# Seven-product projections of a decoder block: two products add into another's PSUM bank, five additions instead of seven, and the first values evicted behind the rates

## The chip, the cores and the metric
The kernel runs on one core of a Trainium2 chip. Five engines work side by side, each through its own instructions in a fixed order, and wait for one another by semaphores: TensorE (PE in the profile, PEld its weight loads), VectorE (DVE), ScalarE (ACT), GpSimd (POOL) and SyncE (SP, which issues most DMAs). PE writes its products into PSUM, here used as eight banks of 128 x 512 float32; DVE and ACT read them from there. The metric is the device time of one execution in microseconds (us), and less is better.

## The reference
One layer of a decoder block, 1024 tokens by 1024 features, all float32:

```python
h = rms_norm(x, pre_mix_norm)
xr, gr, q, k, v, gates = split(h @ w_in)          # widths 1024, 1024, 3 x 1536, 2048
xr = rg_lru(causal_depthwise_conv(xr, conv_w, conv_b), ...)   # gates per block, then a scan over time
y_lru = (xr * gelu(gr)) @ w_lru_proj
q, k = partial_rope(q), partial_rope(k)            # 32 of 128 features of a head are rotated
o = softmax-weighted sum over 3 groups of dilated_window_attention(q, k, v)
y_attn = o @ w_attn_proj
g_lru, g_attn = split(sigmoid(gates))
x = x + rms_norm((g_lru * y_lru + g_attn * y_attn) @ w_out, post_mix_norm)
h = rms_norm(x, pre_ffn_norm)
f = (silu(h @ w_ffn_gate) * (h @ w_ffn_up)) @ w_ffn_down      # width 2816
return x + rms_norm(f, post_ffn_norm)
```

## The kernel before
**Precision.** A float32 operand is split into a high part that PE takes at its fast rate (`hi`, an ACT copy, L98) and the rest (`lo`, a DVE subtraction, L99). A term of a product is three matmuls (`mm3`, L133 to L135): hi by hi, lo by hi, hi by lo. In the profile weights are called `whi` and `wlo`, the layer's normed input and its combinations `hth`/`htl`, `t1`, `t3`, `t4` with h or l behind.

**Quads.** The projections onto xr, gr, q, k and the gates (28 quads, stage 1) and the FFN's gate and up (22 quads) are computed in 2 by 2 blocks with seven products instead of eight. A product is one bank `pq` of 12 matmuls of 128 x 512. The four weight blocks come in two loads (`wraw`); POOL forms their sums `sa` and `sb` (L267 to L270); P1 and P2 take their weights from the first load, P6 and P7 from `sa`, P5 and P3 from `sb`, P4 from a block of the second load (`w4h`, `w4l`). Each pair shares one tile `whi` and one `wlo`, of which there are three. ACT copies P1's bank to `p` (L294), and DVE adds up the rest: u2 = P6 + P1, w = P5 + u2, v = P7 + u2 (tiles `uw`, L309), and the outputs out(0,0) = P2 + P1, out(0,1) = P3 + w, out(1,1) = P7 + w, out(1,0) = P4 + v. An output of stage 1 is the tile `fb` (L720); where there is a function (gelu, sigmoid) ACT applies it to `fb` in place (L722). In the FFN a gate's output is `fo` (L1232, then silu on ACT), and up's is `ut` (L1238), which POOL multiplies into `fo` (L1239). `run_quads` issues a quad as P6, P5, P3, P7, P4 and then P1 and P2 of the next; after each a tick is counted.

**Work between the quads.** The ticks start other work by a table: the units of the LRU (`lru_a`: conv on DVE, L768 and L770, and its split `xch`, `xcl`; `lru_b`: gate matmuls `pgt`, functions on ACT, a scan on DVE) from tick 15 on, every 8; six rotations (`rotate`, L811 to L816; q and k rows `rq` and tables `rcs`, `rsn` come by SP from memory) from tick 146 on, every 5. The weights' second load of a quad waits on SP for its buffer, whose last reader is the split of `w4l`.

**The beginning.** The first half's mean squares (`squares`, L434) give rates (`rates`, L439 to L451: a root on ACT, six small DVE steps, four diagonals `dg`, one matmul `prb` that spreads the rates). Meanwhile the value projection of the first group runs on raw x (banks `bk0`, then `bk1`, `pv`), and `v0_out` (L479) evicts it with the rates as scale. `put` (L425, L426) makes `hth` and `htl`. The same follows for the second half. In the order of the instructions a scheduler has a say; `tc.issue_after(i)` keeps what is inside it behind instruction i on the queue's order. The rotation tables (`rope_tables`) are written to memory from tiles `rot`; the quads' tiles lie in memory that was theirs.

**The FFN's start.** `ORDER` lists steps: t (transposes of a row tile of the normed input), p (weights of a quad's P1 and P2), h (P1, P2 and the copy), x (sums of columns of the input and their splits, L563). Four quads have P1 and P2 ahead of the loop.

Of the kernel before, what the change touches and what calls it, by code (L numbers as in the profile page):

```python
# [41 lines left out]
ORDER = [(s[0], int(s[1])) for s in "t6 h1 p2 p3 x5 h0 t7 x6 x4 h2 x7 h3".split()]  # L42
# [20 lines left out]
def block(ctx, tc, a, out):  # L63
# [169 lines left out]
    class Quad:  # L233
# [47 lines left out]
        def mm(self, p):  # L281
            bank = ps("pq")
# [3 lines left out]
                        xh[:, k, :], xl[:, k, :]) for k in range(4)])  # L286
            return bank

        def start_mm(self):
            self.b = self.mm("P1"), self.mm("P2")  # L290

        def keep(self):
            self.p1 = Quad.pool.tile([128, 512], F32, name="p1", bufs=Quad.P1B)
            A.activation(self.p1, self.b[0], AF.Copy)  # L294

        def head(self):
            self.start_mm()
            self.keep()
# [6 lines left out]
        def body(self):  # L305

            def plus(bank, x):
                y = Quad.up.tile([128, 512], F32, name="uw", bufs=3)
                V.tensor_add(y, bank, x)  # L309
                return y  # L310

            u2 = plus(self.mm("P6"), self.p1)
            yield
            w = plus(self.mm("P5"), u2)
            yield
            self.out(0, 1, self.mm("P3"), w)
            yield
            bank = self.mm("P7")
            self.out(1, 1, bank, w)
            v = plus(bank, u2)  # L320
            yield
            self.out(1, 0, self.mm("P4"), v)
            if self.done:
                self.done()
            yield

    def run_quads(quads, pre, tick=None):
        quads[0].prep()
        for j in range(pre):
            quads[j].first()  # L330
        for j, q in enumerate(quads):
            if j + 1 < len(quads):
                quads[j + 1].prep()
            for _ in q.body():
                if tick:
                    tick()
            if pre <= j + 1 < len(quads):
                quads[j + 1].head()
# [1249 lines left out]
```

## Time and profile before
| | |
|---|---|
| three runs | 1749.28, 1754.31, 1753.51 us; median 1753.51 |
| the profiled execution | 1749.78 us, span 1748.0 us, granted PE clock 0.978 of full speed |
| PE busy | 1676.7 us (96%), 7748 matmuls |
| DVE busy | 1113.9 us (64%) |
| ACT busy | 727.5 us (42%) |
| POOL busy | 698.0 us (40%) |
| chain that ended last | PE 77%, DVE 8%, DMA 5% |

The span is what the profiler saw from the first instruction to the last; the device time lies 1.8 us above it. Busy shares are means over stages that differ. A wait names the engine and line whose result came last.

### The profile page before, as it was taken

Reading aid. Unit: us, or ns where it says so; the run is one execution under the profiler, and the core shown is the slowest. Engines: PE = TensorE matmul, PEld = TensorE weight load, DVE = VectorE, ACT = ScalarE, POOL = GpSimd, SP = SyncE. Lnnn points to the kernel's source line nnn. Section 1 sums busy time; section 2 is a strip of 40 time slices with the busy share of each in tenths; the row PEclk is TensorE's granted clock in tenths of the full one; section 3 lists DMA queues with packets and bytes.
Section 4 is the critical chain, followed back from the end, with each engine's and each line's share of the span. In section 5 each row is a group of like instructions: output and inputs, shape, how many; then the busy total and the mean of one; then the engine's idle time right before and its main releaser. Section 6 shows DMA issues by size and latency. Waiting matters only on the chain.

```text
span 1748.0 us, 21093 instructions
## 1 busy us (share of the span) xinstructions
PE 1676.7 (96%) x7748; PEld 1376.2 (79%) x7748; DVE 1113.9 (64%) x1585; ACT 727.5 (42%) x1130; POOL 698.0 (40%) x650
## 2 busy tenths in 40 slices
PE   8999999999999988989999999799999999999996
PEld 6897888787877876878888887678888888788885
DVE  6966676778788665563433577755545555649658
ACT  6423367554555522464451345422222222344343
POOL 2003354554445434214334204576556566400103
PEclk9899999999999999999999999899999999999998
DMA  8233433333333455584618742133222222475353
GB/s 319 73 133 113 148 133 124 135 137 129 127 133 133 139 166 179 197 330 155 229 50 304 269 162 84 49 115 133 102 103 91 103 91 103 150 261 198 109 186 121
DMA packets 95919, 262.70 MB, mean 150 GB/s; under 512 B 13768, under 2 KB 22120, under 8 KB 94408
## 3 DMA queue, kind: packets, MB, share of 16 engines
q1 hardware_dynamic: 70352, 182.49, 30.7%
q0 software_dynamic: 20352, 76.21, 11.5%
q10 hardware_dynamic: 5112, 2.66, 0.5%
q8 instruction: 61, 1.00, 0.2%
q14 instruction: 42, 0.34, 0.1%
HBM read 180.86 MB, written 80.35 MB: 149 GB/s over the span
## 4 chain that ended last, share of the span: by engine, by line
PE 77%; DVE 8%; DMA 5%; issue 4%; POOL 3%; ACT 2%; SPq 1%; ACTq 0%; DVEq 0%; POOLq 0%
PE pq L135 14%; PE pq L134 14%; PE pq L133 14%; PE pd L1334 4%; PE pd L1335 4%; PE pd L1333 4%; DMA rsn<-rtd 3%; PE py L135 2%; PE py L134 2%; PE py L133 2%; PE pv L463 2%; PE po L1017 2%; PE pv L133 1%; PE pv L135 1%; PE pv L134 1%
## 5 line engine op out<-in xcount | busy, mean ns | idle before, releaser
L135 PE MATMUL pq<-hth,wlo 128*128 128x512 f32 x448 | 179.7, 401 | 9.8 <-DVE wlo L99 9.8
L133 PE MATMUL pq<-hth,whi 128*128 128x512 f32 x448 | 179.6, 401 | 2.8 <-ACT whi L98 2.8
L134 PE MATMUL pq<-htl,whi 128*128 128x512 f32 x448 | 180.7, 403 | 0.0
L267 POOL TENSOR_TENSOR sb<-wraw 128x512 f32<-128x512 f32 x50 | 71.6, 1432 | 173.1 <-DMA wraw<-in_w_fg 92.3
L98 ACT ACTIVATE whi<-sa 128x1024 fp32r<-128x1024 f32 x50 | 53.0, 1059 | 201.5 <-PE pq L134 126.8
L1334 PE MATMUL pd<-fbl,fah 128*128 128x512 f32 x304 | 119.7, 394 | 4.5 <-DVE fbl L99 4.5
L1335 PE MATMUL pd<-fbh,fal 128*128 128x512 f32 x304 | 119.7, 394 | 0.0
L1333 PE MATMUL pd<-fbh,fah 128*128 128x512 f32 x304 | 119.3, 393 | 0.0
L98 ACT ACTIVATE whi<-wraw 128x1024 fp32r<-128x1024 f32 x67 | 70.7, 1055 | 98.2 <-PE pq L134 25.8
L135 PEld LDWEIGHTS pq<-hth,wlo 128*128 128x128 f32 x448 | 86.0, 192 | 32.1 <-DVE wlo L99 11.6
L99 DVE TENSOR_TENSOR wlo<-wraw,whi 128x1024 fp32r<-128x1024 f32 x67 | 91.6, 1367 | 26.4 <-ACT whi L98 23.7
L309 DVE TENSOR_TENSOR uw<-pq,uw 128x512 f32<-128x512 f32 x100 | 68.3, 683 | 60.2 <-PE pq L135 59.5
L133 PEld LDWEIGHTS pq<-hth,whi 128*128 128x128 f32 x448 | 86.0, 192 | 24.7 <-ACT whi L98 3.2
L134 PEld LDWEIGHTS pq<-htl,whi 128*128 128x128 f32 x448 | 85.9, 192 | 20.5
L1407 POOL TENSOR_TENSOR y<-y,gpf 128x512 f32<-128x512 f32 x16 | 25.2, 1602 | 186.9 <-ACT fah L98 109.5
L99 DVE TENSOR_TENSOR wlo<-sa,whi 128x1024 fp32r<-128x1024 f32 x50 | 70.1, 1401 | 28.6 <-ACT whi L98 28.6
L1239 POOL TENSOR_TENSOR fo<-fo,ut 128x512 f32<-128x512 f32 x44 | 60.6, 1381 | 67.1 <-DVE ut L1238 67.1
L720 DVE TENSOR_TENSOR fb<-pq,uw 128x512 f32<-128x512 f32 x84 | 67.8, 807 | 29.4 <-PE pq L135 29.0
L99 DVE TENSOR_TENSOR fal<-ar,fah 128x1024 fp32r<-128x1024 f32 (+1 forms) x41 | 50.5, 1231 | 51.5 <-ACT fah L98 51.4
L98 ACT ACTIVATE fah<-ar 128x1024 fp32r<-128x1024 f32 (+1 forms) x41 | 40.8, 995 | 100.9 <-PE pd L1334 79.5
L133 PE MATMUL pq<-t1h,whi 128*128 128x512 f32 x200 | 79.6, 398 | 0.9 <-ACT whi L98 0.9
L134 PE MATMUL pq<-t1l,whi 128*128 128x512 f32 x200 | 79.4, 397 | 0.0
(542 smaller groups left out, 4948.0 us busy)
## 6 DMA issues: line engine op xcount, KB each, us to landing
ar<-fd SPq DMA_DIRECT2D x35, 512.0 KB
qkd<-fb POOLq DMA_DIRECT2D x24, 512.0 KB, 3.6
qk<-qkd SPq DMA_DIRECT2D x24, 512.0 KB
wraw<-in_w_fg SPq DMA_DIRECT2D x24, 512.0 KB
wraw<-in_w_fu SPq DMA_DIRECT2D x24, 512.0 KB
fd<-fo POOLq DMA_DIRECT2D x11, 1024.0 KB, 4.3
wd<-in_w_dn SPq DMA_DIRECT2D x21, 512.0 KB
fd<-fs POOLq DMA_DIRECT2D x11, 768.0 KB, 5.6
```

The source lines that it names most:

```text
L98: A.activation(hi, src, AF.Copy)
L99: (le or V).tensor_sub(lo, src, f(hi))
L133: T.matmul(o, lh, rh, start=(first and i == 0), stop=False)
L134: T.matmul(o, lh, rl, start=False, stop=False)
L135: T.matmul(o, ll, rh, start=False, stop=(last and i == n - 1))
L267: G.tensor_add(sb[:, lo_], r1[:, lo_], r1[:, hi_])
L309: V.tensor_add(y, bank, x)
L720: V.tensor_add(o, half_in(bank, g), half_in(add, g))
L1239: G.tensor_mul(g, g, ut)
L1333: T.matmul(o, ah[:, ts], bh, start=(i == 0), stop=False)
L1334: T.matmul(o, ah[:, ts], bl, start=False, stop=False)
L1335: T.matmul(o, al[:, ts], bh, start=False, stop=(i == NP - 1))
```

## The change
In a quad P2 now has no bank of its own: it adds into P1's bank once ACT has copied P1, so that bank holds P1 + P2 and needs no addition. P3 adds into P5's bank after out(1,1) has read it. The DVE additions become u2 = P6 + P1, v = P7 + u2, out(1,1) = P5's bank + v, out(1,0) = P4 + v and out(0,1) = P5's bank (with P3) + u2. ACT evicts out(0,0), with its function where there is one; in up's quads DVE multiplies the bank into `fo`. The order of products is P6, P2, P5, P7, P4, the next quad's P1, P3. `ORDER` splits h into a (P1 and its copy) and b (P2). At the beginning four `issue_after` are added and one gets another anchor. PE's matmuls stay the same in number.

```diff
-ORDER = [(s[0], int(s[1])) for s in "t6 h1 p2 p3 x5 h0 t7 x6 x4 h2 x7 h3".split()]
+ORDER = [(s[0], int(s[1])) for s in "t6 a1 p2 p3 x5 a0 b1 t7 x6 x4 a2 b0 x7 a3 b2 b3".split()]
...
+        def head1(self):
+            self.b = self.mm("P1")
         def keep(self):
             self.p1 = Quad.pool.tile([128, 512], F32, name="p1", bufs=Quad.P1B)
+            A.activation(self.p1, self.b, AF.Copy)
...
+        def head2(self):
+            self.mm("P2", self.b)
         def first(self):
             if self.start:
                 self.start()
-            self.out(0, 0, self.b[1], self.p1)
+            self.out(0, 0, self.b, None)
...
     def run_quads(quads, pre, tick=None):
...
+            u2 = plus(q.mm("P6"), q.p1)
+            step()
+            if j >= pre:
+                q.head2()
+                q.first()
+                step()
+            c = q.mm("P5")
+            step()
+            v = plus(q.mm("P7"), u2)
+            q.out(1, 1, c, v)
+            step()
+            q.out(1, 0, q.mm("P4"), v)
+            step()
+            if nxt and j + 1 >= pre:
+                nxt.head1()
+                nxt.keep()
+                step()
+            q.out(0, 1, q.mm("P3", c), u2)
+            if q.done:
+                q.done()
+            step()
...
         else:
-            put(0, j)
-            w0_split(j)
+            with tc.issue_after(last_dve[0].ins):
+                put(0, j)
+                w0_split(j)
...
     r1, rb = rates(ss[1])
-    v0_out(bk0, 0, r0)
+    with tc.issue_after(last_act[0].ins):
+        v0_out(bk0, 0, r0)
...
-    for j in range(4):
-        normed(1, j, rb)
-    for j in range(4):
-        put(0, j)
+    with tc.issue_after(last_dve[0].ins):
+        for j in range(4):
+            normed(1, j, rb)
+        for j in range(4):
+            put(0, j)
...
         def up(n, u, bank, add):
             g = FO[i][:, 2 * n + u, :]
-            ut = op.tile([128, 512], F32, name="ut", bufs=UT)
-            V.tensor_add(ut, bank, add)
-            G.tensor_mul(g, g, ut)
+            if add is None:
+                V.tensor_mul(g, bank, g)
+            else:
+                ut = op.tile([128, 512], F32, name="ut", bufs=UT)
+                V.tensor_add(ut, bank, add)
+                G.tensor_mul(g, g, ut)
```

Three places show how instructions move. The first is ACT between the squares of the second half and its root `rs` (L439, after the change L436): `vs` is an eviction of the first values, `hth` a copy of `put`. Rows of before begin with -, rows after the change with +.

```order
-L479 ACTIVATE vs_393<-pv,rr_287 128x512
-L434 ACTIVATE sq,ss_172<-xn 128x1024
-L479 ACTIVATE vs_393<-pv,rr_287 128x512
-L434 ACTIVATE sq,ss_172<-xn 128x1024
-L479 ACTIVATE vs_393<-pv,rr_287 128x512
-L434 ACTIVATE sq,ss_172<-xn 128x1024
-L479 ACTIVATE vs_393<-pv,rr_287 128x512
-L434 ACTIVATE sq,ss_172<-xn 128x1024
-L425 ACTIVATE hth_120<-x 128x2x512
-L439 ACTIVATE rs_377<-ss_172,epsc 128x4
```
```order
+L422 ACTIVATE hth_120<-x 128x2x512
+L431 ACTIVATE sq,ss_172<-xn 128x1024 x2
+L422 ACTIVATE hth_120<-x 128x2x512
+L431 ACTIVATE sq,ss_172<-xn 128x1024
+L422 ACTIVATE hth_121<-x 128x2x512
+L431 ACTIVATE sq,ss_172<-xn 128x1024
+L422 ACTIVATE hth_121<-x 128x2x512
+L436 ACTIVATE rs_377<-ss_172,epsc 128x4
+L476 ACTIVATE vs_393<-pv,rr_287 128x512 x4
 L98 ACTIVATE whi<-wraw 128x1024 x2
```
The four evictions stood between the squares; they now stand behind the root, and four copies of `put` stand ahead of it instead of one.

The second is PE at the start of stage 1, where P1 and P2 of the first two quads are computed ahead of the loop. Before, the end of the first quad's P1 (bank pq_1418) and the beginning of its P2 (pq_1431):

```order
L133 MATMUL pq_1418<-hth0_120,whi_1414 128x512
L134 MATMUL pq_1418<-htl0_122,whi_1414 128x512
L135 MATMUL pq_1418<-hth0_120,wlo_1415 128x512
L133 MATMUL pq_1431<-hth1_121,whi_1414 128x512 [waits PE_49]
L134 MATMUL pq_1431<-htl1_123,whi_1414 128x512
L135 MATMUL pq_1431<-hth1_121,wlo_1415 128x512
```
After the change, the end of the second quad's P1 (pq_1437) and the beginning of the first quad's P2:

```order
L133 MATMUL pq_1437<-hth0_120,whi_1433 128x512
L134 MATMUL pq_1437<-htl0_122,whi_1433 128x512
L135 MATMUL pq_1437<-hth0_120,wlo_1434 128x512
L133 MATMUL pq_1418<-hth1_121,whi_1414 128x512 [waits Activation_49]
L134 MATMUL pq_1418<-htl1_123,whi_1414 128x512
L135 MATMUL pq_1418<-hth1_121,wlo_1415 128x512
```
P2 waited for a free bank only; now it goes into pq_1418 and waits for ACT's copy of it, and both P1 stand ahead of both P2.

The third is DVE in the last quad that has two rotations in the group from tick 146 on. `rm`, `rq`, `rsn` and `rcs` are the rotation's tiles. Before, from its second rotation's first step on:

```order
L811 TENSOR_TENSOR rm_5480<-rq_5477,rsn 128x512
L814 TENSOR_TENSOR rq_5477<-rq_5477,rcs 128x512
L720 TENSOR_TENSOR fb<-pq,uw 128x512
L99 TENSOR_TENSOR wlo<-sa,whi 128x1024
L813 TENSOR_TENSOR rq_5476<-rq_5476,rcs 128x512
L720 TENSOR_TENSOR fb<-pq,uw 128x512
L309 TENSOR_TENSOR uw<-pq,uw 128x512
L99 TENSOR_TENSOR wlo<-sb,whi 128x1024
L815 TENSOR_TENSOR rq_5476<-rq_5476,rm_5480 128x512
L99 TENSOR_TENSOR w4l<-wraw,w4h 128x512
L720 TENSOR_TENSOR fb<-pq,uw 128x512
L816 TENSOR_TENSOR rq_5477<-rq_5477,rm_5481 128x512
```
After the change, the same rotation:

```order
L814 TENSOR_TENSOR rm_5493<-rq_5490,rsn 128x512
L816 TENSOR_TENSOR rq_5489<-rq_5489,rcs 128x512
L817 TENSOR_TENSOR rq_5490<-rq_5490,rcs 128x512
L818 TENSOR_TENSOR rq_5489<-rq_5489,rm_5493 128x512
L819 TENSOR_TENSOR rq_5490<-rq_5490,rm_5494 128x512
L309 TENSOR_TENSOR uw<-pq,uw 128x512
L99 TENSOR_TENSOR wlo<-sa,whi 128x1024
L723 TENSOR_TENSOR fb<-pq,uw 128x512 x2
L99 TENSOR_TENSOR w4l<-wraw,w4h 128x512
L723 TENSOR_TENSOR fb<-pq,uw 128x512
L99 TENSOR_TENSOR wlo<-sb,whi 128x1024
L309 TENSOR_TENSOR uw<-pq,p_5487 128x512
```
The rotation's steps were mixed with the additions; they now stand together ahead of v (the first `uw`), out(1,1) and the next quad's splits.

## Rows read from the trace of the kernel before
**Rows 1.** The page, busy time of each engine with its share of the span and its instructions.
```profile
PE 1676.7 (96%) x7748; PEld 1376.2 (79%) x7748; DVE 1113.9 (64%) x1585; ACT 727.5 (42%) x1130; POOL 698.0 (40%) x650
```
**Rows 2.** Table of windows: the stretch in us, its length, then for PE, PEld, DVE, ACT and POOL the busy time and in brackets the instructions, then the granted PE clock, the DMA share and GB/s.
```profile
39.00:62.00 23.00, 16.05 (x56) 11.83 (x55) 18.00 (x28) 7.10 (x9) 0.64 (x1) 0.78 0.26 92
50.00:75.00 25.00, 25.00 (x137) 21.63 (x136) 22.91 (x24) 10.81 (x14) 1.45 (x2) 0.95 0.13 43
157.00:169.00 12.00, 8.31 (x28) 6.07 (x27) 6.05 (x7) 5.24 (x7) 7.08 (x6) 0.86 0.25 87
175.00:600.00 425.00, 417.78 (x1768) 334.09 (x1767) 324.92 (x389) 237.70 (x292) 206.56 (x168) 0.99 0.37 131
430.00:446.00 16.00, 12.38 (x42) 9.28 (x41) 10.12 (x9) 6.96 (x9) 4.45 (x5) 0.79 0.16 55
600.00:704.00 104.00, 94.16 (x381) 74.46 (x380) 57.83 (x78) 28.38 (x40) 42.89 (x43) 0.93 0.56 182
1084.00:1124.00 40.00, 28.73 (x105) 21.84 (x104) 35.10 (x34) 19.78 (x33) 26.77 (x18) 0.79 0.13 44
1160.00:1516.00 356.00, 356.00 (x1555) 291.72 (x1554) 191.89 (x205) 99.51 (x129) 215.90 (x164) 1.00 0.28 102
```
**Rows 3.** Waits of PE: line and product, what it waited for, us in all, times, the longest.
```profile
PE pq L135 <- DVE wlo L99: 11.4, 6, 4.7
PE pq L133 <- ACT whi L98: 10.0, 4, 5.7
PE pgt L133 <- ACT xch L98: 3.9, 3, 2.2
```
**Rows 4.** Groups of instructions by line and shape, of DVE and POOL: busy us and mean ns, then the idle time before them.
```profile
L309 DVE TENSOR_TENSOR uw<-pq,uw 128x512 f32<-128x512 f32 x100 | 68.3, 683 | 60.2 <-PE pq L135 59.5
L720 DVE TENSOR_TENSOR fb<-pq,uw 128x512 f32<-128x512 f32 x84 | 67.8, 807 | 29.4 <-PE pq L135 29.0
L99 DVE TENSOR_TENSOR wlo<-sa,whi 128x1024 fp32r<-128x1024 f32 x50 | 70.1, 1401 | 28.6 <-ACT whi L98 28.6
L1239 POOL TENSOR_TENSOR fo<-fo,ut 128x512 f32<-128x512 f32 x44 | 60.6, 1381 | 67.1 <-DVE ut L1238 67.1
```
**Rows 5.** Timeline of DVE, ACT and PE, 20 to 48 us: start, duration, engine, line, operation; in brackets the idle time before it and what ended it.
```profile
22.10 0.17 DVE L441 RECIPROCAL rr<-rs 128x4 f32<-128x4 f32 x1
22.97 0.87 DVE L449 TENSOR_SCALAR dg<-cst,re 128x128 f32<-128x128 f32 x4
32.14 0.69 ACT L479 ACTIVATE vs<-pv,rr 128x512 f32<-128x512 f32 x1 [5.28 <-PE pv L463]
32.73 1.05 ACT L434 ACTIVATE sq<-xn 128x1024 f32<-128x1024 f32 x1
38.60 1.06 ACT L425 ACTIVATE hth<-x 128x1024 fp32r<-128x1024 f32 x1
39.55 0.29 ACT L439 ACTIVATE rs<-ss,epsc 128x4 f32<-128x4 f32 x1
40.84 0.17 DVE L441 RECIPROCAL rr<-rs 128x4 f32<-128x4 f32 x1
45.73 0.86 DVE L449 TENSOR_SCALAR dg<-cst,re 128x128 f32<-128x128 f32 x4
46.74 2.04 PE L451 MATMUL prb<-dg,ones 128*128 128x512 f32 x2 [6.95 <-DVE dg L449]
```
**Rows 6.** Timeline of ACT and PE at the start of the quads.
```profile
156.61 1.09 ACT L294 ACTIVATE p<-pq 128x512 f32<-128x512 f32 x2 [5.10 <-DMA rtd<-rot]
160.16 0.50 PE L133 MATMUL pq<-hth,whi 128*128 128x512 f32 x1 [2.75 <-ACT whi L98]
```
**Rows 7.** Timeline of PE and DVE in a quad beside the LRU.
```profile
549.79 0.39 PE L135 MATMUL pq<-t3h,wlo 128*128 128x512 f32 x1
555.81 0.40 PE L134 MATMUL pq<-htl,whi 128*128 128x512 f32 x1
558.14 0.39 PE L135 MATMUL pq<-hth,wlo 128*128 128x512 f32 x1
559.41 0.51 PE L133 MATMUL pgt<-xch,gw 128*128 128x512 f32 x1 [0.88 <-ACT xch L98]
558.56 1.07 DVE L720 TENSOR_TENSOR fb<-pq,uw 128x512 f32<-128x512 f32 x1
```
**Rows 8.** Group of DVE's L811 by shape, and two rows of DVE's timeline in the stretch of the rotations.
```profile
L811 DVE TENSOR_TENSOR rm<-rq,rsn 128x512 f32<-128x512 f32 x6 | 6.4, 1070 | 36.3 <-DMA rsn<-rtd 36.3
651.93 0.68 DVE L99 TENSOR_TENSOR w4l<-wraw,w4h 128x512 fp32r<-128x512 f32 x1
663.43 0.69 DVE L811 TENSOR_TENSOR rm<-rq,rsn 128x512 f32<-128x512 f32 x1 [8.06 <-DMA rsn<-rtd]
```
**Rows 9.** Timeline of DVE at the start of the FFN.
```profile
1099.29 1.78 DVE L563 TENSOR_TENSOR b22l<-h2f,b22h 128x512 fp32r<-128x512 f32 x1
1110.69 0.68 DVE L563 TENSOR_TENSOR b22l<-h2f,b22h 128x512 fp32r<-128x512 f32 x1
1111.30 0.68 DVE L1232 TENSOR_TENSOR fo<-pq,p 128x512 f32<-128x512 f32 x1
1111.90 1.21 DVE L99 TENSOR_TENSOR wlo<-sa,whi 128x1024 fp32r<-128x1024 f32 x1
```

More of the change, by code (lines that the diff above doesn't have):

```diff
@@ L128, in h_tiles, with mm3 @@
         return ts, [ts[k // 4][:, k % 4, :] for k in range(KT)]
-    def mm3(o, terms, first=True, last=True):
+    def mm3(o, terms, first=True, last=True, **kw):
         n = len(terms)
         for i, (lh, ll, rh, rl) in enumerate(terms):
-            T.matmul(o, lh, rh, start=(first and i == 0), stop=False)
-            T.matmul(o, lh, rl, start=False, stop=False)
-            T.matmul(o, ll, rh, start=False, stop=(last and i == n - 1))
+            T.matmul(o, lh, rh, start=(first and i == 0), stop=False, **kw)
+            T.matmul(o, lh, rl, start=False, stop=False, **kw)
+            T.matmul(o, ll, rh, start=False, stop=(last and i == n - 1), **kw)
     def gain_bc(ap, name, eng=None, mk=None):
@@ L279, in prep, with mm @@
             self.w["P4"] = h4, l4
-        def mm(self, p):
-            bank = ps("pq")
+        def mm(self, p, bank=None):
+            first = bank is None
+            bank = bank or ps("pq")
             wh, wl = self.w[p]
@@ L302, in first, with plus @@
                 self.start()
-            self.out(0, 0, self.b[1], self.p1)
[L305 to L325, printed above, removed]
-    def run_quads(quads, pre, tick=None):
+            self.out(0, 0, self.b, None)
+    def run_quads(quads, pre, tick=None):
+        def plus(bank, x):
+            y = Quad.up.tile([128, 512], F32, name="uw", bufs=3)
+            V.tensor_add(y, bank, x)
+            return y
+        step = tick or (lambda: None)
         quads[0].prep()
@@ L331, in run_quads @@
         for j, q in enumerate(quads):
[L332 to L338, printed above, removed]
[L339 to L343 removed]
+            nxt = quads[j + 1] if j + 1 < len(quads) else None
+            if nxt:
+                nxt.prep()
+            u2 = plus(q.mm("P6"), q.p1)
[19 more added lines that the diff above has]
+            step()
     rtd = dp.tile([NG, 2, 16, S], F32, name="rtd")
@@ L1060, in block @@
         q1[j].keep()
+    for j in range(PRE1):
+        q1[j].head2()
     def open_ep():
@@ L1311, in x_cols, with head @@
         x_sums(t, h2f, x2, XB, XB)
+    def head(j):
+        quads[j].head1()
+        quads[j].keep()
     for step, j in ORDER:
-        {"p": pre, "h": lambda q: quads[q].head(), "t": e_turn, "x": x_cols}[step](j)
+        {"p": pre, "a": head, "b": lambda q: quads[q].head2(), "t": e_turn, "x": x_cols}[step](j)
     h2ctx.close()
```

31 lines of the change are left out of this document (12 added, 19 removed).

## The prediction
> **What bounds the kernel now.** I read the page first: TensorE (PE) is busy 96% of the 1748.0 us span [rows 1]. The change adds and removes no matmul, so the only time it can win is time in which PE waits or runs at a low clock. Then the table of windows, for the stretches where that happens [rows 2]. In a clean stretch one matmul follows the next after (558.14 − 555.81)/10 = 0.233 us [rows 7]; in the feed-forward part (FFN) it is 356/1555 = 0.229 us [rows 2]. A window's length less its matmuls times that pitch is what PE lost there, low clock included (a lost record makes the figure a little too large):
> rates of the norm, 39 to 62: 23 − 56 × 0.233 = 10.0 us;
> start of the quads, 157 to 169: 12 − 28 × 0.233 = 5.5;
> quads beside the LRU, 175 to 600: 425 − 1768 × 0.233 = 13.1, nearly half of it (6.2) in 430 to 446;
> quads beside the rotations, 600 to 704: 104 − 381 × 0.233 = 15.2;
> start of the FFN, 1084 to 1124: 40 − 105 × 0.229 = 16.0.
> Together 60 us: the field on which this change plays. The reader should see next that the waits that end these idle times name VectorE's (DVE's) low parts of weights and ScalarE's (ACT's) high parts [rows 3]: DVE is the engine that comes late. In 1160 to 1516, 19 quads long, PE has no gap and DVE works 191.89 of 356 us [rows 2].
>
> **The additions.** A quad loses two DVE additions of the kinds that took 683 and 807 ns [rows 4], about 1.4 us. Fifty quads give 70 us of DVE time, and ACT takes over one eviction in the 16 quads that have no function of their own. The FFN's 22 quads (31 us of the 70) have nothing to give: PE never waits there, and DVE is half idle. POOL loses 11 products of 1381 ns [rows 4], hidden in the same stretch. I count 0, with 0 to +3 for the moved P2 and P3.
> So only the 28 quads of the first stage can win, and there PE's order gets tighter. P3 may not start before DVE has read P5's bank in out(1,1); between P7's end and P3 only P4 and the next P1 run, 24 matmuls or 5.6 us. The low part of the P5/P3 weights likewise has only the 12 matmuls of the next P6 between its slot's release and its use, since P3 is now the quad's last product. In the kernel before no product shares a bank, and an addition may come later than that at no cost.
>
> **Beside the LRU (−8 to +12, taken as 0).** How late DVE can be there: the last matmul of a P7 (its x is t3) began at 549.79, so the product was done at 550.2; the addition out(1,1) that reads its bank started at 558.56 [rows 7]. These 8.4 us are beyond the 5.6 that P3 will allow. DVE is busy 324.92 of 425 us [rows 2], and its conv, scan and splits stand in line between the additions. Less work by 1.4 us per 19.6 us of PE time (7 × 12 × 0.233) shortens that queue; the new wait punishes what is left of it. If all the additions' relief arrived at PE, some 8 of the 13.1 us could go (the rest is the gate's own chain, as at 559.41, where PE waits for ACT [rows 7]). If P3 waited 2 us in four quads, with a low clock behind each, +12.
> **Beside the rotations (−7 to +8, taken as +0.5).** DVE stands 36.3 us in six waits for the table rsn [rows 8]: its load is issued behind SP's second weight load, which waits for w4l. From w4l's start (651.93) to L811 (663.43) it took 11.5 us. DVE's work from there to the next w4l is 10 short operations and two wlo after the change, 12 and two before. At 0.61 us apart for a short one and 1.2 for a wlo the loop is 11.5 + 8.5 = 20 us instead of 21, and PE needs 19.6: nearly half of the 15.2 us could go. But the last quad of the group carries two rotations ahead of v and out(1,1); six more DVE operations and a second wait for rsn come before P3, some 4 to 6 us with the clock behind it. I let these cancel.
>
> **The rates (−10 to 0, taken as −0.6).** After the first reciprocal the chain to the end of dg took 22.10 to 23.84, 1.7 us; the second time 40.84 to 46.59, 5.8 us, since four splits stand between its links [rows 5]. Now the chain runs unbroken. ACT, however, has three more hth copies (1.06) and four fewer evictions (0.69) ahead of rs [rows 5]: from about 32.4 on four squares of 1.05 with their read-out and four copies make 8.4 us, so rs ends near 41.2 rather than 39.84, dg near 43.2, and PE starts 3.4 us earlier. What is saved isn't kept: PE runs without a gap from there, and the splits that were between the links now stand behind them, on a DVE that is busy 22.91 of 25 us in 50 to 75 [rows 2]. A product there will wait for its low half instead. I keep a fifth of the 3.4.
> **Start of the quads (0 to +4, taken as +2.2).** ACT's first copy of a P1 bank began at 156.61 after 5.10 us of waiting for the DMA out of rot, whose memory p1 takes over [rows 6]. Before, PE had P1, P2, P1, P2 to do until 157.4 and didn't notice. Now P2 writes into the bank that this copy reads. P1 of both quads ends two products (5.6 us) earlier, at 151.8, so PE stands from there to about 157.2. That puts back the 5.6 us of P2s; the wait that is there now, 2.75 us until 160.16 [rows 6], and its echo vanish behind them. 5.5 of idle and about 2.5 of low clock against the 5.5 lost now: +2.5, less a little that the rates bring.
> The Trainium skill ("TensorE: Matmul & The Clock Gate", HAM oscillation) says that an idle PE falls to 1.2 GHz and that activity brings 2.4 GHz back; were both P2s to run at the low level, their 24 matmuls would take 5.6 us more and the term would be +5.6. The trace shows less: after 6.95 us of idle at 46.74 [rows 5] the whole window lost 10.0, so the low clock took 3.0, at a granted clock of 0.78 [rows 2].
> **Start of the FFN (−1 to +3, taken as +0.9).** DVE sets the pace: a row of 20 splits up to 111.30, then an addition of 0.68 and the sums' wlo at 1111.90 [rows 9]. That addition goes (−0.6). ORDER splits the heads in two, so one more wlo falls among the splits (+1.2) and P2s that PE did in the shadow come behind (+0.3).
> The Trainium skill ("SBUF — State Buffer", who interferes with whom) has it that a DVE operation with two SBUF inputs blocks against a POOL operation that reads SBUF. By that the added wlo could cost 2.3 here, and the removed additions, one input of which is PSUM, were the cheap ones. The split of 1.78 us at 1099.29 against 0.68 at 1110.69 [rows 9] bears this out; the term would be +2.
>
> **Sum.** −0.6 + 2.2 + 0 + 0.5 + 0.9 + 0 = +3.0 on the profiled execution's 1749.78 us: 1752.8. That execution lies at the low end of the runs (1749.28 to 1754.31, median 1753.51), so 1753 is as good as no change. About 0.3%, 5.3 us, is what a measurement of this kernel can tell.
>
> **The rivals.**
> *Relief arrives* (faster). DVE's 1.4 us per quad empties its queue, P3's wait is never last, and the LRU and rotation stretches give back 8 and 7 of their 28 us; with the rest as above, 1749.78 + 3.0 − 15.5 = 1737. For it: 11.4 us of PE's waits for pq name DVE's wlo [rows 3]. Against it: the rsn loop is a DMA's, and the longest LRU wait, 2.2 us, names ACT's xch [rows 3], which comes behind the conv, not behind an addition. Chance 0.32.
> *P3 waits* (slower). out(1,1) comes more than 5.6 us behind P7 in the quads where conv or rotation stands ahead of v. It decides as soon as that happens in five or more of some twenty quads: each costs 1 to 2 us of idle and about 1.5 of low clock, 5 × 3 = +15, so 1765. For it: the 8.4 us delay at 558.56 [rows 7], and the double rotation. Against it: the delay shrinks with the work. Chance 0.31.
> *The rates' gain is kept whole*: 3.4 of idle and the 3 us of low clock behind it go, 1752.8 − 5.8 = 1747, still within 0.3% of the run; it belongs to "same" and has 0.08 of its 0.37.
> *Nothing is felt*, as PE sets the time everywhere: 1750; the terms then are below what can be told, also "same".
> **Numbers.** No change has 0.37, with a range of its own of 1748 to 1758; faster has 0.32 and slower 0.31, by the first two rivals. The range of 8 in 10 reaches to both: 1737 to 1767.
>
> **What would show it.** Right: idle before the first P2 near 152 to 157, releaser ACT's copy; PE's prb 2 to 4 us earlier and a new wait for a low half before 157; waits of P3 for DVE's out(1,1) in 300 to 704; FFN quads without a gap as now. Wrong: no wait of P3 at all and a windows table with under 10 us lost in 175 to 704 (the first rival), or over 45 (the second). A wait of the next P6 or P5 for wlo in the FFN would break my zero there.

## The result: 0.7% slower, 1765.4 us
The median is 1765.40 us (1762.84 to 1770.06, five runs) against 1753.51 us (1748.91 to 1758.84, five runs) for the kernel before. The ratio is 1.0073, 95% interval 1.0045 to 1.0102, some 13 us. The forecast, no change at 1753 with a range of 1748 to 1758, was wrong; the time is that of the second rival, P3 waits (1765). The profiled execution took 1765.4 us, span 1763.4 us, granted clock 0.977.

The page after, busy time by engine (before: [rows 1]):
```profile
PE 1678.4 (95%) x7748; PEld 1378.0 (78%) x7748; DVE 1078.2 (61%) x1496; ACT 734.6 (42%) x1147; POOL 685.8 (39%) x639
```
The table of windows after (columns as in [rows 2]; windows are moved with the stages):
```profile
39.00:62.00 23.00, 21.82 (x96) 17.43 (x97) 22.02 (x28) 8.96 (x12) 2.29 (x3) 0.93 0.27 92
175.00:600.00 425.00, 417.01 (x1776) 334.65 (x1775) 301.43 (x348) 245.16 (x308) 202.30 (x170) 0.99 0.38 133
600.00:708.00 108.00, 91.22 (x355) 71.28 (x354) 61.64 (x69) 26.75 (x38) 44.58 (x42) 0.91 0.53 171
```
PE's waits after (columns as in [rows 3]):
```profile
PE pq L135 <- DVE wlo L99: 14.5, 5, 4.4
PE pq L133 <- DVE fb L723: 13.5, 6, 3.7
PE psc L904 <- DMA qk<-qkd: 10.3, 1, 10.3
PE pT L1214 <- DVE xnw L195: 9.5, 2, 8.6
PE pq L133 <- ACT p L296: 6.0, 2, 5.5
```
DVE's busy time fell by 36 us and not by the 70 that were counted. The additions that went are 64 us by their groups (in eleven quads of up a DVE product takes an addition's place), and other steps, the same in number, took longer; the largest part of that is in the low parts `wlo` from `wraw`, before and then after (why they are longer isn't shown):
```profile
L99 DVE TENSOR_TENSOR wlo<-wraw,whi 128x1024 fp32r<-128x1024 f32 x67 | 91.6, 1367 | 26.4 <-ACT whi L98 23.7 <-PE pT L1208 1.4
L99 DVE TENSOR_TENSOR wlo<-wraw,whi 128x1024 fp32r<-128x1024 f32 x67 | 105.4, 1575 | 63.9 <-ACT whi L98 60.7 <-PE pq L135 1.6 <-PE pT L1214 1.4
```
PE is no better for the 36 us. Its waits for `xch` [rows 3] are gone from the list, as are most for `whi`. In their place stand the second line, P3 waiting for out(1,1), the last one, P2 waiting for ACT's copy, and, larger than before, the waits for `wlo`, for the attention's `qk` (6.6 us before) and for `xnw` (3.4 before).

Where the 15.4 us between the two spans lie is read by laying the traces side by side: a quad is 84 matmuls into `pq`, so the end of the 84th, 168th, ... can be compared. Lengths of the stages in us, each from one profiled execution:

| kernel | to end of quad 1 | quads 2-21 (LRU) | 22-26 (rotations) | end of stage 1 to 2nd FFN quad | next 20 FFN quads | rest |
|---|---|---|---|---|---|---|
| before | 171.6 | 427.2 | 113.4 | 375.9 | 386.4 | 231.1 |
| after | 171.2 | 425.5 | 123.6 | 385.2 | 387.2 | 228.3 |
| difference | -0.4 | -1.7 | +10.2 | +9.3 | +0.8 | -2.8 |

(Quads 27 and 28 take 42.4 in both.) From the end of stage 1 to the last matmul of the projections behind the attention (`py`) it is 221.8 before and 227.8 after: of the 9.3 us 6.1 lie there and 3.2 at the start of the FFN. Three places, then, and only the first and the last were in the sum.

**The rotations.** DVE's timeline after, at the first two rotations, and PE's answer to it (columns as in [rows 5]):
```profile
609.65 0.69 DVE L814 TENSOR_TENSOR rm<-rq,rsn 128x512 f32<-128x512 f32 x1 [6.70 <-DMA rsn<-rtd]
...
616.10 1.21 DVE L99 TENSOR_TENSOR wlo<-wraw,whi 128x1024 fp32r<-128x1024 f32 x1
617.24 0.68 DVE L814 TENSOR_TENSOR rm<-rq,rsn 128x512 f32<-128x512 f32 x1
...
622.67 0.68 DVE L309 TENSOR_TENSOR uw<-pq,uw 128x512 f32<-128x512 f32 x1
...
624.40 1.28 DVE L723 TENSOR_TENSOR fb<-pq,uw 128x512 f32<-128x512 f32 x2
```
```profile
617.37 0.79 PE L135 MATMUL pq<-hth,wlo 128*128 128x512 f32 x1 [3.51 <-DVE wlo L99]
...
625.14 0.79 PE L133 MATMUL pq<-hth,whi 128*128 128x512 f32 x1 [3.72 <-DVE fb L723]
```
DVE stands 6.70 us before L814 for `rsn`, and the low part of the next quad's P1 and P2 (616.10) stands behind the whole rotation. It could have run at about 606, since ACT's high part was there at 605.89. Before, it did, ahead of the wait:
```profile
605.29 1.23 DVE L99 TENSOR_TENSOR wlo<-wraw,whi 128x1024 fp32r<-128x1024 f32 x1
612.88 0.69 DVE L811 TENSOR_TENSOR rm<-rq,rsn 128x512 f32<-128x512 f32 x1 [6.37 <-DMA rsn<-rtd]
```
So P1 waits 3.51 us. The second rotation then stands ahead of v (622.67) and out(1,1) (624.40), and P3 waits 3.72 us. Both waits are followed by matmuls at the low clock (granted 0.60 in the 4.0 us from 617.4 on, 0.50 in the 3.9 us from 625.1 on): quad 22 takes 24.8 us instead of 19.6, quad 23 26.2 instead of 20.0.

In quads 24 and 25 P1 waits for its `wlo` as well, but there PE had waited before the change too, for the `wlo` of P6. Before, then after:
```profile
649.13 0.80 PE L135 MATMUL pq<-hth,wlo 128*128 128x512 f32 x1 [4.68 <-DVE wlo L99]
674.56 0.79 PE L135 MATMUL pq<-hth,wlo 128*128 128x512 f32 x1 [3.68 <-DVE wlo L99]
```
```profile
668.17 0.62 PE L135 MATMUL pq<-hth,wlo 128*128 128x512 f32 x1 [3.37 <-DVE wlo L99]
693.95 0.79 PE L135 MATMUL pq<-hth,wlo 128*128 128x512 f32 x1 [4.38 <-DVE wlo L99]
```
These quads take 24.7 and 26.3 us, against 26.4 and 26.3 before. The 10.2 us are those of quads 22 (+5.2) and 23 (+6.2), less 1.7 in quad 24 and with 0.6 more in quad 26.

**The attention.** SP's timeline, after and then before:
```profile
762.63 1.94 SPq L109 DMA_DIRECT2D lraw<-ld  x4
764.61 2.08 SPq L109 DMA_DIRECT2D qk<-qkd  x4
```
```profile
740.19 10.59 SPq L109 DMA_DIRECT2D lraw<-ld  x8
750.82 7.23 SPq L109 DMA_DIRECT2D qk<-qkd  x4
```
PE's wait for these loads, before and then after:
```profile
762.71 3.62 PE L901 MATMUL psc<-qk 128*128 128x128 f32 x16 [5.53 <-DMA qk<-qkd]
```
```profile
775.51 0.77 PE L904 MATMUL psc<-qk 128*128 128x128 f32 x2 [10.29 <-DMA qk<-qkd]
```
Four of the LRU results' loads (`lraw`) go into the memory of `hth1`, which P3 reads. P3 was the last quad's third product and is now its last: it ends at 762.60, the loads are issued at 762.63, and the `qk` loads behind them on SP 13.8 us later than before, though stage 1 ends 8.0 us later only. PE's wait for `qk` grows from 5.5 to 10.3 us.

That this edge is worth all of the 6.1 us isn't shown. Among the experiments below, the kernels with P3 last take 226.4 to 230.1 us from the end of stage 1 to the last `py`, and seven of the nine that have P3 third in the last quad, the kernel before among them, take 221.4 to 222.5; but the other two (experiments 1 and 9) took 228.5 and 227.7 in their profiled executions. So some 6 us can come there without the edge.

**The FFN's start.** DVE and POOL after, DVE before, and PE after:
```profile
1095.93 4.00 DVE L184 SCALAR_TENSOR_TENSOR rq<-rr,rv 128x1 f32<-128x1 f32 x1
1094.98 2.49 POOL L566 TENSOR_TENSOR x<-h2f,h2f 128x512 f32<-128x512 f32 x2
1097.43 2.47 POOL L566 TENSOR_TENSOR h2f<-h2f,x 128x512 f32<-128x512 f32 x2
```
```profile
1082.43 1.10 DVE L184 SCALAR_TENSOR_TENSOR rq<-rr,rv 128x1 f32<-128x1 f32 x1
```
```profile
1101.84 0.45 PE L1214 MATMUL pT<-cst,xnw 128*128 128x128 f32 x1 [8.57 <-DVE xnw L195]
```
A step of 128 x 1 (L184, in the chain to `xnw`) took 4.00 us: it ended at 1099.93, when POOL's four subtractions in a row were done (1099.90). Before, a `wlo` stood ahead of it and it took 1.10. PE's wait for `xnw` went from 2.5 to 8.57 us; against that, a wait of 5.72 us for `whi` at 1106.68 before is one of 0.95 us at 1123.11 after. In all seven kernels with the change's list of steps L184 takes 3.99 or 4.00 us here, in the seven with the old list 1.10 or 1.11; from the last `py` to the end of the second quad it is 157.4 to 160.3 us in the former and 153.7 to 156.2 in the latter. The Trainium skill ("SBUF — State Buffer", Who interferes with whom) says that DVE and GpSimd share a pair of ports under an exclusive lock; the trace agrees, with 4.00 against 0.22 us for the same step while POOL rests.

### The profile page after: what moved, and what is told of

It reads as the page before. It is cut to its first block, busy times and chain, and to the rows that moved or that the text cites. A ratio compares the mean times of both kernels' runs of the same rounds, so it can differ in the third digit from the quotient of the medians.

```text
span 1763.4 us, 20916 instructions
## 1 busy us (share of the span) xinstructions
PE 1678.4 (95%) x7748; PEld 1378.0 (78%) x7748; DVE 1078.2 (61%) x1496; ACT 734.6 (42%) x1147; POOL 685.8 (39%) x639
## 4 chain that ended last, share of the span: by engine, by line
PE 62%; DVE 7%; DMA 4%; issue 2%; ACT 1%; POOL 1%; SPq 1%; DVEq 0%; POOLq 0%; ACTq 0%
PE pq L133 12%; PE pq L134 11%; PE pq L135 11%; PE pd L1348 4%; PE pd L1349 4%; PE pd L1347 4%; PE py L135 2%; PE py L134 2%; PE py L133 2%; DMA rsn<-rtd 2%; PE po L1020 2%; DVE wlo L99 1%; PE pe L134 1%; PE pe L135 1%; PE pe L133 1%
## 5 line engine op out<-in xcount | busy, mean ns | idle before, releaser
L133 PE MATMUL pq<-hth,whi 128*128 128x512 f32 x448 | 182.9, 408 | 19.0 <-DVE fb L723 13.5
L99 DVE TENSOR_TENSOR wlo<-wraw,whi 128x1024 fp32r<-128x1024 f32 x67 | 105.4, 1575 | 63.9 <-ACT whi L98 60.7
L269 POOL TENSOR_TENSOR sa<-wraw 128x512 f32<-128x512 f32 x50 | 69.2, 1384 | 142.0 <-DVE fo L1239 31.7
L309 DVE TENSOR_TENSOR uw<-pq,uw 128x512 f32<-128x512 f32 x50 | 34.4, 688 | 103.2 <-PE pq L135 103.2
L99 DVE TENSOR_TENSOR wlo<-sb,whi 128x1024 fp32r<-128x1024 f32 x50 | 74.2, 1484 | 24.9 <-ACT whi L98 24.8
L267 POOL TENSOR_TENSOR sb<-wraw 128x512 f32<-128x512 f32 x50 | 67.9, 1358 | 44.1 <-DVE wlo L99 17.3
L1249 POOL TENSOR_TENSOR fo<-fo,ut 128x512 f32<-128x512 f32 x33 | 52.7, 1597 | 74.4 <-DVE ut L1248 54.7
L99 DVE TENSOR_TENSOR wlo<-sa,whi 128x1024 fp32r<-128x1024 f32 x50 | 64.1, 1281 | 26.8 <-ACT whi L98 26.8
```

The lines of the kernel that those rows point to most:

```text
L99: (le or V).tensor_sub(lo, src, f(hi))
L133: T.matmul(o, lh, rh, start=(first and i == 0), stop=False, **kw)
L267: G.tensor_add(sb[:, lo_], r1[:, lo_], r1[:, hi_])
L269: G.tensor_sub(sa[:, hi_], r0[:, lo_], r1[:, lo_])
L1249: G.tensor_mul(g, g, ut)
```

## The experiments
Ratios are to the kernel before on the same chip, with 95% intervals; the medians of the kernel before were 1754.3 to 1755.0 us, so 0.001 is 1.75 us.

**1. The rates' edits alone** (in the kernel before: three `issue_after` are added, not four as told with the change, and a fourth gets another anchor).
```
-            put(0, j)
-            w0_split(j)
+            with tc.issue_after(last_dve[0].ins):
+                put(0, j)
+                w0_split(j)
...
+    with tc.issue_after(last_act[0].ins):
+        v0_out(bk0, 0, r0)
...
```


> The kernel before with the edits of the first stage alone (evictions of the first values behind the rates, the four places of issue_after); quads and ORDER as before. The trace of the changed kernel reached the first P1 of the quads 2.8 us earlier. Theory A (these 2.8 us are the rates' own and stay): PE idle before prb falls from 6.95 to about 3.0 us, the quads start 2.8 us earlier, and with P1 and P2 in the old order the wait for ACT's copy at the start stays away: 1750.5 us, ratio 0.998. Theory B (my prediction's step: given back to a later wait for a low half): ratio 1.000 and the first P1 no earlier than 0.6 us.


Measured: 1751.88 us, 0.9982 (0.9964 to 0.9999). A gain, near 3 us (0.2 to 6.3 by the interval). It isn't the loss. In the profiled execution, with 1757.3 us the longest of the twelve, the wait before `prb` falls from 6.95 to 3.00 us as theory A says, but the first P1 begins at 145.34 instead of 146.03 only, near theory B's 0.6: where the gain lies isn't shown.

**2. P3 with a bank of its own** (in the kernel after).
```
+            w = plus(c, u2)
...
-            q.out(0, 1, q.mm("P3", c), u2)
+            q.out(0, 1, q.mm("P3"), w)
```


> The changed kernel, but P3 goes into a bank of its own again and w = P5 + u2 is formed by DVE (six additions a quad); order of products, P2 in P1's bank and all else as changed. Theory A (the loss beside the LRU and the rotations is P3's wait for out(1,1)): the six waits of P3 for DVE's output, 13.5 us in all in the changed kernel, are gone, the stretch 600 to 708 takes 5 to 8 us less, and the time is 1752 to 1757 us against 1765.4. Theory B (DVE is late there because of its own work; one more addition of 0.7 us makes it later, and the wait moves to wlo): 1762 to 1768 us.


Measured: 1764.16 us, 1.0060 (1.0039 to 1.0080). Its waits of PE:
```profile
PE pq L135 <- DVE wlo L99: 18.8, 6, 5.8
...
PE pgt L133 <- ACT xch L98: 5.0, 2, 2.7
```
No product waits for `fb` any more, 13.5 us less, and 4.3 us more stand at `wlo` and 5.0 at `xch`. The shared bank names the wait; it isn't what makes DVE late. The edit also gives DVE one addition more per quad, so it doesn't tell the price of the shared bank by itself. The rotations still take 121.3 us.

**3. The last `lraw` loads into other memory** (in the kernel after, two allocations exchanged).
```
-    lraw += [rbuf("lraw", "r2") for _ in range(4)]
     lTl = [rbuf("lTl", "r3", F32R) for _ in range(4)]
+    lraw += [rbuf("lraw", "r2") for _ in range(4)]
```


> The changed kernel with the four last loads of lraw in the memory of htl0, last read by P6 of the last quad, rather than that of hth1, last read by P3 (two lines of allocation exchanged). Theory A (SP stands 16 us in these loads until the last product, P3, has read hth1, and the loads of q and k of the second group stand behind them): SP issues them at 747 instead of 763, the loads of qk follow at about 752, the wait of psc for qk falls from 10.3 to 5 us or less, and the time is 1759 to 1761 us. Theory B (the wait of psc is set by the rotated rows or by PE's own delay of 8 us): wait unchanged, 1764 to 1767 us.


Measured: 1768.39 us, 1.0084 (1.0065 to 1.0102).
```profile
PE py L133 <- ACT lTh L98: 5.5, 1, 5.5
```
The time is above both theories. SP's `lraw` loads no longer wait for P3 and the wait for `qk` is gone, but this one is there instead. ACT's first copy `lTh` begins 1.3 us behind the end of stage 1, here (766.91) as in the kernel after (763.90); before, it began 2.8 us ahead of that end (751.77). The exchange freed the loads and not the copies; what holds these isn't shown.

**4. The relief alone** (order and banks of before, five additions per quad; w and the additions of P1 into out(0,0) and of P5 into out(0,1) and out(1,1) are left out).
```
-            w = plus(self.mm("P5"), u2)
+            self.mm("P5")
...
-            self.out(0, 1, self.mm("P3"), w)
+            self.out(0, 1, self.mm("P3"), u2)
...
-            self.out(0, 0, self.b[1], self.p1)
+            self.out(0, 0, self.b[1], None)
...
```


> The kernel before, order of products and banks as before, but with five additions a quad: out(0,0) is ACT's eviction of P2's bank without P1, w is not formed and u2 stands in its place (the product P5 is still made, its bank is not read). So part of the sums is left out of the outputs, no matmul is. It shows what two additions less are worth to the old order, with no shared bank. Theory A (relief is worth what PE waits for DVE's queue): the waits for pgt beside the LRU and for wlo beside the rotations shrink, 28 us lost there become 13 to 20, the time is 1738 to 1746 us. Theory B (the gate's chain and the DMA loop of the rotations bind, not the additions): 1750 to 1755 us.


Measured: 1750.46 us, 0.9977 (0.9966 to 0.9989).
```profile
PE pq L135 <- DVE wlo L99: 12.2, 5, 4.9
```
Two additions fewer are worth 4 us, and none of it at the rotations: that stage takes 113.7 us (113.4 before), and the wait for `wlo` is as long as in [rows 3]. So the loop over `rsn` there isn't shortened by these additions taken from DVE. Where the 4 us lie, the one profiled execution (span 1749.2) doesn't show.

**5. The rotations behind the next quad's low part** (in the kernel after; `last_a` is the last `wlo` of a P1 and P2, and all five DVE steps of a rotation stay behind it).
```
...
+        with tc.issue_after(last_a[0].ins):
             V.tensor_mul(m1, t2, sn)
             V.tensor_mul(t1, t1, cs)
...
```


> The changed kernel, but the DVE operations of a rotation are kept behind the split of the next quad's P1/P2 weights (wlo from wraw) in DVE's order; loads, POOL's share and all else as changed. In the changed kernel this split stands behind the rotation's first operation, which waits for the DMA of rsn. Theory A (that place in the order costs the 10 us beside the rotations: P1 waits for the low half, and behind a second rotation P3 waits for out(1,1)): the waits for wlo at 617, 668 and 694 (11.3 us) and the two of P3 (5.5 us) fall to 4 us or less in all, 600 to 708 loses 3 to 8 us instead of 25, and the time is 1748 to 1756 us against 1765. Theory B (the slots or P3's shared bank cost it, wherever the rotation stands): out(1,1) is now behind the wait for rsn, P3 waits longer, 1762 to 1768 us.


Measured: 1756.47 us, 1.0010 (0.9996 to 1.0023). The order of DVE in the first rotation quad is as meant (lines move a little with an edit: L819 here is L814 after):
```profile
606.99 1.22 DVE L99 TENSOR_TENSOR wlo<-wraw,whi 128x1024 fp32r<-128x1024 f32 x1 [2.97 <-ACT whi L98]
610.73 0.69 DVE L819 TENSOR_TENSOR rm<-rq,rsn 128x512 f32<-128x512 f32 x1 [2.51 <-DMA rsn<-rtd]
```
```profile
PE pq L134 <- DVE fb L726: 18.6, 7, 6.9
...
PE pq L136 <- DVE wlo L99: 3.6, 2, 2.4
```
Waits for `wlo` fall from 14.5 to 3.6 us, P3's rise from 13.5 to 18.6, and the stage takes 110.6 us, 13.0 less than after and 2.8 less than before. The time falls by 9 us (11 by the ratios), the largest single part of the loss. The stage agrees in every kernel made: 121.3 to 125.8 us in the five that have the rotations as the change has them, 110.6 to 113.0 in the five with this edit.

**6. The last quad of stage 1 in the old order** (in the kernel after): P3, with its own bank, directly behind P5.
```
+            if tick and nxt is None:
+                w = plus(c, u2)
+                q.out(0, 1, q.mm("P3"), w)
...
```


> The changed kernel, but the last quad of stage 1 makes P3 behind P5, in a bank of its own, with w = P5 + u2, as the kernel before does; so hth1 and htl1 are read for the last time two products earlier, and P4 is the last product. Theory A (SP and ACT stand until the last product has read hth1 and htl1, and the loads of q and k stand behind): SP issues the later loads of lraw 5 to 6 us earlier, the wait of psc for qk or of py for lTh falls from 10.3 to 5 us, time 1759 to 1761 us. Theory B (the attention is late by the delay that PE brings with it): 1764 to 1767 us.


Measured: 1764.30 us, 1.0048 (1.0032 to 1.0065).
```profile
770.26 0.98 PE L911 MATMUL psc<-qk 128*128 128x128 f32 x3 [4.83 <-DMA qk<-qkd]
```
The wait for `qk` falls from 10.29 to 4.83 us, as theory A says, and the stage behind it from 385.2 to 381.4 (to the last `py` from 227.8 to 221.5). The time alone couldn't tell it: its interval overlaps with that of the kernel after.

**7. Another list of steps at the FFN's start** (in the kernel after).
```
-ORDER = [(s[0], int(s[1])) for s in "t6 a1 p2 p3 x5 a0 b1 t7 x6 x4 a2 b0 x7 a3 b2 b3".split()]
+ORDER = [(s[0], int(s[1])) for s in "t6 a1 p2 p3 x5 a0 b1 b0 t7 x6 x4 a2 x7 a3 b2 b3".split()]
```


> The changed kernel with P2 of the FFN's first quad (b0) put ahead of the last transposes (t7) in ORDER instead of behind the columns' sums. Theory A (at the FFN's start PE lost 3 us because its P2s no longer fill the wait for xnw): the idle time before the last transposes falls from 8.6 to about 5.8 us and the first quads end 2.5 to 3 us earlier, 1762 to 1763 us. Theory B (DVE's row of splits sets the end of this stage, with one more wlo in it wherever P2 stands): 1764 to 1767 us.


Measured: 1769.90 us, 1.0084 (1.0063 to 1.0105): no gain.
```profile
1106.37 0.87 PE L1214 MATMUL pT<-cst,xnw 128*128 128x128 f32 x3 [8.58 <-DVE xnw L195]
```
The wait for `xnw` is the same, and L184 takes 4.00 us here too. Where this P2 stands in the list doesn't matter to it; that it is what stands on DVE ahead of L184 that matters is argued from the rows, not shown.

**8. P2 shared in another place** (kernel before with the rates' edits; the next quad's P1 ahead of P4, its P2 into P1's bank behind P4, P3 as before, six additions).
```
...
+            if nxt:
+                nxt.head1()
...
             self.out(1, 0, self.mm("P4"), v)
...
+            if nxt:
+                nxt.head2()
...
```


> The kernel before with the rates' edits, and of the quads' change only P2 in P1's bank, in another place: P6, P5, P3, P7, next P1, P4, next P2. P3 has its bank, w is formed (six additions), the four and two quads ahead of the loops are as before. Theory A (what cost time was P2 so late that its weights' slot is released late, and P3 last; an addition less is worth about 2 us, the rates 3): 1748 to 1751 us against 1755 for the kernel before. Theory B (any product that waits for ACT's copy costs): copy and P4 don't overlap, 1755 to 1765 us.


Measured: 1752.90 us, 0.9987 (0.9975 to 0.9999), no better than the rates alone.
```profile
PE pq L133 <- ACT p L295: 18.2, 6, 7.9
```
Here P2 stands one product behind the copy that it waits for, and that copy is late beside the rotations: they take 120.1 us.

**9. and 10. Edits 5 and 6 together; then also old heads** (P1 and P2 of the two and the four quads ahead of the loops adjacent, with a bank of its own for P2, and the old `ORDER`; `pa` is p1 for these quads and nothing for the others).
```
+        def head12(self):
+            self.b, self.b2 = self.mm("P1"), self.mm("P2")
...
-            self.out(0, 0, self.b, None)
+            self.out(0, 0, self.b2, self.pa)
...
```


> The changed kernel with two of its parts put right at once: the rotations' DVE steps stay behind the next quad's low part of P1 and P2, and the last quad of the first stage is issued in the old order, with a bank of its own for P3. Theory A, the two losses are separate and add: 9 to 10 us from the rotations and 1 to 5 from the attention's start, so 1751 to 1755 and a ratio to the kernel before of 0.998 to 1.001; PE's wait for the qk loads near 5 us and no wait for a low part in 600 to 704. Theory B, what is won at the rotations is lost again at the next stage, whose loads are timed from the same stage's end: 1756 or more, as with the rotations alone.

> The kernel with both parts put right, and besides the quads that stand ahead of a loop (two of the first stage, four of the feed-forward part) keep P1 and P2 adjacent, with a bank of its own for P2 and the old list of steps. Theory A, the heads cost what the trace says, 2.4 us at the start of the quads and 3 us at the start of the feed-forward part: 4 to 6 us less than the kernel without this edit, so 1746 to 1750 and a ratio of 0.994 to 0.998; PE's wait for xnw back to about 2.5 us. Theory B, the waits there move to the next dependence (the copy that waits for the DMA out of rot, the row of splits): within 2 us of the kernel without it.


Measured: 1748.05 us, 0.9964 (0.9951 to 0.9977), and 1746.13 us, 0.9943 (0.9922 to 0.9964). The two losses add, and more comes than was expected; both kernels beat the kernel before. The traces don't show where: in that of number 9 the length to the last `py` is 227.7 us, as in the kernel after, in an execution of 1752.63 us. With the heads, the stage that holds the FFN's start takes 377.1 us instead of 385.6, but 6.3 of these 8.5 lie ahead of the last `py`, where the heads change nothing, and 2.2 behind it; L184 and the wait for `xnw` are back at 1.11 and 2.47 us. The first quad ends at 171.5 instead of 170.2. The two intervals overlap, so the heads' price in time is open.

**11. and 12. Only the FFN's heads in the old order; then P3's own bank on top** (edit 2).


> Only the feed-forward part's four quads ahead of the loop keep P1 and P2 adjacent, with a bank of its own for P2 and the old list of steps; the two quads ahead of the first stage's loop are as in the changed kernel. Rotations and last quad of the first stage are put right as in the two kernels before. Theory A, of the two heads only the feed-forward one costs anything (the trace of the kernel with both heads in the old order shows it 1.3 us later at the end of the first quad and about 8 us earlier in the feed-forward part): 1744 to 1746 and a ratio of 0.993 to 0.995. Theory B, the start of the quads is worth the 2.4 us that the changed kernel's trace put on it: 1748 and 0.996.

> The same kernel, and P3 has a bank of its own in every quad, with w = P5 + u2 formed for it: one addition more on DVE per quad, and no product waits for out(1,1) any more (19 us in the trace of the kernel with the heads put right). Theory A, with the rotations out of the way the shared bank is what is left of the loss: 5 to 12 us less than the same kernel with the shared bank, so 1733 to 1740. Theory B, DVE is late for the next wait as well (pgt's xch, the low part of P5's and P3's weights), as it was when this edit was made to the changed kernel: within 3 us.


Measured: 1745.92 us, 0.9950 (0.9932 to 0.9968), and 1745.84 us, 0.9942 (0.9921 to 0.9964). Waits of PE of 11:
```profile
PE pq L134 <- DVE fb L739: 19.4, 7, 7.4
...
PE pq L134 <- ACT p L303: 5.4, 1, 5.4
```
and of 12:
```profile
PE pq L136 <- DVE wlo L99: 10.5, 5, 5.0
...
PE pgt L134 <- ACT xch L98: 4.5, 2, 2.4
```
Number 11 is the kernel after with three pieces of order put right, and it is some 19 us faster than that: the ledger of rotations, attention and FFN start (10.2 + 6.1 + 3.2) as a whole, though not term by term. Its stages are 171.8, 428.0, 110.9, 377.9, 387.1 and 228.3 us. The start of the quads stays as the change has it, with its wait of 5.4 us for the copy of P1, and costs nothing that can be told: old heads there gave 1746.13 against 1745.92. In 12 the 19.4 us of P3's waits vanish, 10.5 us at `wlo` (2.2 in 11) and 4.5 at `xch` stand in for part of them, and the time stays; theory B again. By the stages its own bank helps beside the LRU (422.3 instead of 428.0) and hurts at one place of the FFN (390.1 instead of 387.1); a bank of its own in stage 1 alone wasn't tried.

## Why the prediction was wrong, step by step
**The frame held, the relief was counted too high.** PE works the same 7748 matmuls, and what it lost lies in its waits and the clock behind them. The stretches that it listed are those in which most of it lies; the attention and the last stage were missing. Of the 70 us that the additions were to free on DVE, 36 came.

**The step that failed is the rotations' (+0.5, measured +10.2).** It set a gain of "nearly half of the 15.2" from a shorter loop against a loss of 4 to 6 us from the double rotation and let them cancel. The gain doesn't exist: with two additions fewer and the old order the stage takes as long as before (experiment 4). The loss was sought at one place, the last double rotation, where it is small: five DVE steps come there and not six, L814 follows at 693.82 without a second wait for `rsn`, P3 waits 1.81 us at 700.39, and the quad takes 0.6 us longer than before. The same order stands at the first double rotation, in quad 23, with 3.72 us of wait and 6.2 us of quad. And one row ahead of those that the document shows for the change stands the next P1's `wlo`, slipped behind the rotation and its wait for `rsn`: in quad 22 that is 3.51 us of a wait that PE didn't have before, and 5.2 us of quad. Experiment 5 puts this one edge right and gets 9 us; that it takes quads 24 and 25 below the kernel before as well (29.1 and 19.6 us, together 4.1 less) is part of them. The bound of +8 was too narrow for both places together.

**A term was missing: the attention (+6.1).** The sum followed the engines' instruction order and the queues beside the quads, not the last quad's buffers into the next stage. P3, moved from third to last, is the last reader of memory that SP's next loads wait for; the prediction's own rule for a moved step, that each queue it is moved past counts, would have found it. Experiment 6 shows the edge, as PE's wait for `qk` halves with it; experiment 3 shows that the loads are not all of it. The size of +6.1 is one trace's and can come without the edge (above).

**The FFN's start (+0.9, measured +3.2).** The mechanism named, DVE against POOL on SBUF, was right; the place was not. The step held up is one of 128 x 1 on the chain to `xnw`, by 2.9 us more than before, and not the added `wlo`; PE's longer wait for `xnw` is in part made good by the shorter one for `whi`.

**The rates (-0.6, measured -3.1 by experiment 1, -6.3 to -0.2 by its interval).** The new waits came as told:
```profile
40.18 1.04 PE L448 MATMUL prb<-dg,ones 128*128 128x512 f32 x1 [3.03 <-DVE dg L446]
```
```profile
73.11 0.50 PE L133 MATMUL pv<-whi,hth 128*128 128x256 f32 x2 [1.75 <-ACT whi L620]
74.81 0.58 PE L134 MATMUL pv<-wlo,hth 128*128 128x256 f32 x1 [1.20 <-DVE wlo L621]
```
But `prb` came 6.6 us earlier, not 3.4: ACT's `hth` copies went into time in which it had waited for PE (5.28 us in [rows 5]), so the root ended at 38.25 instead of the reckoned 41.2. How much of the 6.6 survives the two waits of 1.75 and 1.20 us differs by trace: the first P1 begins at 143.18 to 145.34 in the kernels with the new rates, at 146.03 before. So it isn't kept whole, as the rival had it; a fifth is likely too little, but the interval doesn't exclude it.

**The start of the quads (+2.2).** The wait is there:
```profile
154.48 0.80 PE L133 MATMUL pq<-hth,whi 128*128 128x512 f32 x1 [5.52 <-ACT p L296]
153.83 1.08 ACT L296 ACTIVATE p<-pq 128x512 f32<-128x512 f32 x2 [5.16 <-DMA rtd<-rot]
```
The trace puts 2.4 us on it (the first P1 2.8 us earlier, the end of the first quad 0.4), but that is luck: with the old heads the quads begin no earlier. The end of the first quad lies between 170.0 and 172.0 us in all kernels that have the new rates, whichever heads they have, and at 171.6 before.

**What held.** The LRU's 0 (-1.7: waits for `xch` went, P3's of 2.90, 0.94, 0.55 and 3.60 us came). The FFN's 0 to +3: each quad takes 19.31 instead of 19.25 us, and does so in every kernel in which P2 adds into P1's bank, whether P3 shares a bank or not. The last stage became 2.8 us shorter, which no term had and no experiment explains.

**The rival that hit** was right in its time by luck and half right in its cause. P3 waits six times, 13.5 us, and at 625.14 with a price in the quad; but experiments 2 and 12 take those waits away and the time stays, and experiment 5 leaves 18.6 us of them and gets 9 us. Its bound, lost time over 45 us in 175 to 704, wasn't reached either: by the forecast's own pitch, 425 - 1776 x 0.233 = 11.2 and 108 - 355 x 0.233 = 25.3, together 36.5 against 28.3 before.

**Open.** Where the relief's 4 us and the rates' 3 lie; why the other half of the relief on DVE went into longer steps; and the size of the attention's part in time, which is 1 to 4 us by experiment 6 (medians, ratios) and 8 by 9 against 5, with intervals that meet, while the traces of experiments 1 and 9 have its 6 us without its cause.

## What to carry to other kernels
When a product is moved, list for each engine's queue what now stands behind a wait on a DMA, and for each buffer that the product reads who is waiting for its last reader: the loss at the rotations and the later `qk` loads were such edges, and neither was arithmetic. A wait that is named in the list isn't yet the cause; take it away, and if the time stays and the wait shows up at the next name, look for the engine that is late and for what it stands behind. Work saved on an engine that waits for a DMA need not be time saved: the rotations took 113.7 us with two additions fewer, 113.4 with them.

## What was not expected of the hardware
**The same wait can be followed by either clock.** P3's wait of 1.81 us behind the same instructions, in the kernel after and in experiment 3, each with the window behind it:
```profile
700.39 0.50 PE L133 MATMUL pq<-hth,whi 128*128 128x512 f32 x1 [1.81 <-DVE fb L723]
700.40:706.50 6.10, 6.10 (x26) 4.96 (x27) 3.25 (x5) 3.25 (x5) 0.60 (x1) 1.00 0.77 211
```
```profile
700.79 0.79 PE L133 MATMUL pq<-hth,whi 128*128 128x512 f32 x1 [1.81 <-DVE fb L723]
700.80:706.50 5.70, 5.70 (x13) 4.45 (x14) 1.32 (x3) 2.19 (x4) 0.60 (x1) 0.50 0.76 220
```
In the first the matmuls follow 0.23 us apart at a granted clock of 1.00 (2.4 GHz), in the second 0.43 us apart at 0.50 (1.2 GHz) until 706.5, and the quad takes 24.3 instead of 21.7 us. So this wait cost itself in one execution, and 2.6 us more in the other; the two kernels differ in two allocations only, so it is taken for a difference between executions, though no kernel was profiled twice. The kernel before, unchanged, ran between 1746.4 and 1761.6 us in the 80 executions beside the experiments, and a sum made against one profiled execution is no finer than that. The Trainium skill ("TensorE: Matmul & The Clock Gate", Part 1: The HAM clock gate) says that the number of cold matmuls, those at the low clock, varies from run to run of one kernel, for the kernel's start; here the two traces differ so behind a wait in its middle.

**A 128 x 1 step can take 4 us** beside POOL (above), against 0.22 us at rest, and did in all seven kernels with the change's list: in the kernel after it ended when POOL's row of operations did.
